# One more Strassen pair in the second half of an attention output projection, and a memory load moved to a later step

## The chip, the cores and the metric

The kernel runs on one core of a Trainium2 chip. The core has five engines that each work through a queue of their own in order: TensorE (PE, matrix products into PSUM), VectorE (DVE) and ScalarE (ACT) for elementwise work, GpSimd (POOL) and SyncE (SP), which here mainly send DMA transfers. The metric is device microseconds (us) of one execution. Before the change the median of 3 runs is 2434.72 us (2434.51 to 2436.06).

## The reference

One residual block of an encoder, 256 tokens by 2048 features, all in float32: a SwiGLU feed-forward net, a mixer, a cross attention to 256 memory tokens, a second feed-forward net, each followed by a layer norm. The change lies at the end of the mixer, where its two attention branches A and B are projected, gated, added and projected again, and in the layer norm of the memory that is prepared beside it:

```python
g_a, g_b = jnp.split(g, 2, axis=-1)                  # sigmoid gates, 256 x 2048 each
y_b = mla_attention(...) @ w_o_b                      # 256 x 2048 by 2048 x 2048
mix = (g_a * y_a + g_b * y_b) @ w_out
h = layer_norm(ALPHA * h + mix)
m = layer_norm(mem, mem_ln_g, mem_ln_b)               # keys and values of the cross attention
```

## The kernel before

**Precision.** Every float32 operand is split into a rounded part `hi` and a rest `lo`; a product is three matmuls (hi hi, hi lo, lo hi). ScalarE makes `hi` of a weight tile by two casts of 1024 columns (L264), VectorE makes `lo` by a subtraction over all 2048 columns (L267). A weight tile is 128 x 2048 (1 MB), loaded by SyncE into one of three `raw` buffers (L193); two `hi` and two `lo` buffers hold the parts. A buffer is reused when its last reader has finished, so a load waits for the subtraction of the tile three before, and a cast for TensorE two tiles back.

**Pairs and groups.** `pair_group` computes a 256 x 1024 piece of a projection. One weight tile holds two tiles of the inner dimension (a pair) for two blocks of 512 output columns. The inner dimension of 2048 makes eight pairs, called 0 to 7 here. A plain pair (`mm_pair`, L311) is 2 inner tiles x 2 token halves x 2 column blocks x 3 = 24 matmuls of 512 columns. A Strassen pair (`mm_sums`, L366) makes the same products with 7 instead of 8 block products, 21 matmuls. For it VectorE adds weight blocks into a stage tile (L248 over 1024 columns, L250 twice over 512), ScalarE casts it in two halves (L264, `H5<-X3`), VectorE subtracts it (L267, `X2<-X3,H5`); the tile's own `hi` and `lo` then span 1536 columns. It also needs a `form`, sums of the activations (`sum_forms`, L321 and L325, split at L255 and L256), kept either in a named block or in four small work tiles, which are soon reused. Its shared results collect in four extra PSUM banks, the other four than those of the group's plain results; `shared` (L679 to L684) combines them.

**B's projection.** `out_b(g)` runs two groups, g = 0 and 1. The table `AT_YB` says which pairs are Strassen pairs: 2, 4 and 6 in the first group, 4 and 6 in the second. The forms of 4 and 6 lie in block T0; that of 2 lies in work tiles. The activations of B lie in blocks T2 (pairs 0, 1), T3 (2, 3), H4 (4, 5) and T1 (6, 7). After a group `done` (L1282 to L1284) adds the shared results, multiplies by the gate and adds branch A; plane copies (L846, ScalarE), DMA transposes (L850, SyncE) and joins (L854, L255, L256) then turn the result into blocks for the next projection. The first group's turning runs beside the second group; the second group's runs beside `w_out`, whose first pairs read the first group's blocks X0 and X1.

**Memory.** `mem_norm` returns steps that are woven between the pairs of the `w_out` groups. Step 0 loads the memory as tokens (two 1 MB tiles into T1 and T2) and turned (two 1 MB tiles into T3 and H4), all from GpSimd's queue. Each waits until B's second group has read the block. Steps 10 to 14 use the turned memory.

**Order.** The program states the work in one sequence with priorities; a scheduler that models the engines places each instruction in its engine's queue when the program is built. So an added instruction can also change the order of its neighbours.

Of the kernel before, what the change touches and what calls it, by code (L numbers as in the profile page):

```python
# [30 lines left out]
            {3: ("X1", 0), 5: ("X1", 1), 7: ("X0", 0)})  # L31
SUMS_GATE, AT_GATE = {**SUMS_IN, 5: ("F", 0)}, ((2, 4, 5, 6), (2, 4, 5, 6), (2, 4, 6), (2, 4, 6))
ORDER_GATE = (0, 2, 1, 4, 5, 3, 6, 7)
SUMS_YB = {4: ("T0", 0), 6: ("T0", 1), 2: None}
AT_YB = (2, 4, 6), (4, 6)
SUMS_XQ = {4: ("H5", 0), 6: ("H5", 1), 2: None}
SUMS_XV = {4: ("T3", 0), 6: ("T3", 1), 2: None}
SUMS_XO = {2: None, 4: ("H2", 0), 6: ("H2", 1)}
# [63 lines left out]
class Kernel:  # L102
# [767 lines left out]
    def mixer(self, xT, st, steps):  # L870
# [403 lines left out]
        def out_b(g):  # L1274
# [21 lines left out]
            def turn(n):  # L1296
                def fn():
                    mix.blocks += self.act([("X0", "X1", "T0", "X3")[2 * g + n]]).blocks
                    for tt in range(2):
# [4 lines left out]
                return fn  # L1304
            self.pair_group(g, t["w_o_b"][g], 512, KT, lambda: oB["t"], AT_YB[g], fb, ps, qs, None,
                            (("H5", "X2"), "X3"))
# [8 lines left out]
        for c in (2, 4, 6):  # L1315
            self.add(self.forms_step(fb, SUMS_YB, c, lambda: oB["t"]))
        side = out_b(0)
# [13 lines left out]
    def mem_norm(self):  # L1331

        nc, t = self.nc, self.t
        e = self.mem = {}

        def load():
            e["m"] = [self.block(f"T{1 + tt}", (P, D)) for tt in range(2)]
            e["raw"] = [self.block(g) for g in ("T3", "H4")]
            for j in range(2):
                nc.gpsimd.dma_start(e["m"][j], t["mem"][j])  # L1340
            for j in range(2):
                nc.gpsimd.dma_start(e["raw"][j], t["memT"][:, 8 * j:8 * j + 8, :])

        def stat(tt):
            def fn():
                if tt == 0:
                    e["diag"] = self.w2((P, 4, P))
                    e["ones"] = self.w1((P, P))
                    nc.gpsimd.memset(e["ones"], 1.0)
                st = self.ln_begin()  # L1350
                with self.tc.issue_after(self.last_lo.ins):
                    for n in range(4):
                        self.ln_piece(st, e["m"][tt], n)
                kept = self.chain
                mean, r, _ = self.ln_scale(st)
                self.chain = kept
                for k, v in enumerate((mean, r)):
                    nc.vector.tensor_scalar(e["diag"][:, 2 * k + tt, :], self.ident, v, None, ALU.mult)
                if tt:
                    e["mT"] = self.act(["H0", "H1", "H2", "H3"])  # L1360
            return fn

        def spread():

            ps = self.at_tile()
            with self.tc.issue_after(self.last_mm.ins):
                for j in range(4):
                    nc.tensor.matmul(ps[:, j * P:(j + 1) * P], e["ones"], e["diag"][:, j, :], start=True, stop=True)
            e["mr"] = self.w2((P, 2, 1, S))
            nc.scalar.copy(e["mr"].rearrange("p a o s -> p (a o s)"), ps)  # L1370

        def quarter(q):
            def fn():
                v = e["raw"][q // 2][:, q % 2 * 4:q % 2 * 4 + 4, :]
                for k, op in enumerate((ALU.subtract, ALU.mult)):
                    nc.vector.tensor_tensor(v, v, e["mr"][:, k].to_broadcast([P, 4, S]), op)
                for j in range(4):
                    kt = 4 * q + j
                    nc.scalar.activation(v[:, j, :], v[:, j, :], AF.Identity,
                                         bias=self.vec("mem_ln_b", kt), scale=self.vec("mem_ln_g", kt))  # L1380
                self.split(v, e["mT"].blk(0, 4 * q, 4), e["mT"].blk(1, 4 * q, 4))
            return fn

        return {0: [load], 4: [stat(0)], 7: [stat(1)], 9: [spread], 10: [quarter(0)], 11: [quarter(1)], 13: [quarter(2)], 14: [quarter(3)]}

    def turned_norm(self, ln, st, x):

# [289 lines left out]
def _pairs(u, g, n, turned):  # L1677


    import numpy as np  # L1680
    k, c = u.shape
    w = np.stack([m.reshape(k // P, P, c // n, n) for m in (u, g)])
    for j in range(c // n):
        for i in turned[j]:
            w[:, 2 * i:2 * i + 2, :, j] = w[::-1, 2 * i:2 * i + 2, :, j].copy()
    return w.transpose(3, 2, 1, 0, 4).reshape(c // n, P, k // P * 2 * n)


def _halves(w):

    w = w.reshape(w.shape[0], -1, 2, 512)
    return [w[:, :, i].reshape(w.shape[0], -1) for i in (0, 1)]
# [6 lines left out]
def _layout(i):  # L1699
# [39 lines left out]
    r["w_o_a"] = _pairs(*_halves(a["w_o_a"][0]), 512, [(), ()])  # L1739
    r["w_o_b"] = _pairs(*_halves(a["w_o_b"][0]), 512, AT_YB)  # L1740
    r["w_out"] = _pairs(*_halves(a["w_out"][0]), 512, [(), ()])
# [35 lines left out]
```

## Time and profile before

| | |
|---|---|
| Median of 3 runs | 2434.72 us |
| The profiled execution | 2432.88 us, of which the span of the instructions is 2431.0 us |
| TensorE busy | 2422.4 us |
| VectorE busy | 2131.3 us (88%) |
| ScalarE busy | 1553.1 us (64%) |
| B's second group on TensorE | 1241.62 to 1283.78 us |
| Granted TensorE clock | 1.0 of full speed |

The busy time of TensorE is modelled from its queue, so "100%" says that it never stood empty for long, not that it runs at its peak. What another engine's time costs is read from the stretch in which it works and from who waits for whom there.

### The profile page before, as it was taken

The page shows a single profiled execution, that of the slowest core. Times are in us where ns is not written, and L with a number is a line of the kernel's source. Part 1 is how long each engine was busy: PE and PEld are TensorE (multiplying, and loading weights), DVE is VectorE, ACT ScalarE, POOL GpSimd, SP SyncE. Part 2 cuts the span into 40 slices and gives each one's busy share as a digit, 9 for nine tenths or more (in the row PEclk, how much of TensorE's full clock was granted, in tenths as well). Part 3 has the DMA queues.
Part 4 walks back from the last instruction along what each step waited for, and adds up shares of the span by engine and source line. Part 5 has one row for each costly group of instructions (what it writes and reads, how often), then busy time and mean ns, then how long its engine had stood idle before and what let it go on. Part 6 is the DMA issues. An engine that isn't in the chain of part 4 may idle for free.

```text
span 2431.0 us, 29704 instructions
## 1 busy us (share of the span) xinstructions
PE 2422.4 (100%) x11280; PEld 2021.5 (83%) x11280; DVE 2131.3 (88%) x2437; ACT 1553.1 (64%) x2022; POOL 36.0 (1%) x81
## 2 busy tenths in 40 slices
PE   9999999999999999999999999999999999999999
PEld 8888888889888888888888888888888888888887
DVE  8999989899889998789788889879879999888997
ACT  6676745666555557878565787755666675556662
POOL 0000000000000001000000000000000000000000
PEclk9999999999999999999999999999999999999999
DMA  7766656667645657776577577655556766666665
GB/s 267 253 211 215 206 201 223 210 202 230 218 174 211 216 202 242 236 203 176 186 254 246 170 237 214 216 183 192 191 199 213 228 222 211 219 207 207 201 222 180
DMA packets 176416, 516.21 MB, mean 212 GB/s; under 512 B 111729, under 2 KB 112497, under 8 KB 121105
## 3 DMA queue, kind: packets, MB, share of 16 engines
q1 hardware_dynamic: 170816, 495.83, 61.5%
q0 software_dynamic: 4592, 17.30, 2.3%
q8 instruction: 88, 1.44, 0.2%
q10 hardware_dynamic: 864, 1.18, 0.1%
q14 instruction: 56, 0.45, 0.1%
HBM read 485.30 MB, written 2.10 MB: 200 GB/s over the span
## 4 chain that ended last, share of the span: by engine, by line
PE 89%; DVE 4%; ACT 3%; DMA 2%; issue 1%; SPq 0%; DVEq 0%; ACTq 0%
PE at L311 25%; PE mm L311 24%; PE at L366 11%; PE mm L366 11%; PE mm L298 10%; PE mm L277 4%; PE mm L279 2%; DVE lo L267 2%; ACT hi L264 2%; PE at L1034 1%; DMA raw<-w_xq 1%; DMA raw<-w_xk 0%; DMA raw<-w_xv 0%; PE at L1088 0%; ACT w L832 0%
## 5 line engine op out<-in xcount | busy, mean ns | idle before, releaser
L264 ACT CAST hi<-raw 128x1024 fp32r<-128x1024 f32 (+1 forms) x852 | 803.4, 980 | 440.4 <-PE at L311 130.5
L267 DVE TENSOR_TENSOR lo<-raw,hi 128x2048 fp32r<-128x2048 f32 (+1 forms) x427 | 902.2, 2115 | 136.1 <-ACT hi L264 129.1
L311 PE MATMUL mm<-hi,T 128*128 128x512 f32 (+1 forms) x1312 | 308.1, 384 | 0.5 <-ACT hi L255 0.4
L264 ACT CAST X<-H 128x1024 fp32r<-128x1024 f32 (+1 forms) x170 | 174.7, 1034 | 171.5 <-DVE H L248 117.5
L311 PEld LDWEIGHTS mm<-hi,T 128*128 128x128 f32 x1312 | 244.4, 188 | 46.8 <-ACT hi L255 0.9
L311 PE MATMUL at<-hi,T 128*128 128x512 f32 x1136 | 272.3, 390 | 0.0
L311 PEld LDWEIGHTS at<-hi,T 128*128 128x128 f32 x1136 | 213.3, 188 | 44.4
L267 DVE TENSOR_TENSOR X<-H,X 128x2048 fp32r<-128x2048 f32 (+1 forms) x85 | 191.5, 2253 | 62.1 <-ACT X L264 61.9
L311 PE MATMUL mm<-lo,T 128*128 128x512 f32 (+1 forms) x656 | 158.1, 383 | 0.0
L311 PE MATMUL at<-lo,T 128*128 128x512 f32 x568 | 141.0, 390 | 0.0
L311 PEld LDWEIGHTS mm<-lo,T 128*128 128x128 f32 x656 | 122.2, 188 | 22.4
L311 PE MATMUL at<-hi,H 128*128 128x512 f32 x560 | 133.4, 390 | 0.0
L311 PEld LDWEIGHTS at<-lo,T 128*128 128x128 f32 x568 | 106.7, 188 | 22.1
L311 PEld LDWEIGHTS at<-hi,H 128*128 128x128 f32 x560 | 105.0, 188 | 21.5
L250 DVE TENSOR_TENSOR H<-H,raw 128x512 f32<-128x512 f32 (+1 forms) x170 | 115.7, 681 | 2.4
L311 PE MATMUL mm<-hi,H 128*128 128x512 f32 x480 | 115.6, 392 | 0.4 <-DVE w L684 0.4
L311 PEld LDWEIGHTS mm<-hi,H 128*128 128x128 f32 x480 | 89.6, 188 | 19.5 <-DVE w L684 0.8
L248 DVE TENSOR_TENSOR H<-raw 128x1024 f32<-128x1024 f32 (+1 forms) x85 | 102.2, 1203 | 0.5 <-DMA raw<-w_gate 0.3
L366 PE MATMUL mm<-X,X 128*128 128x512 f32 x342 | 91.3, 392 | 0.0
L264 ACT CAST X<-raw 128x1024 fp32r<-128x1024 f32 (+1 forms) x54 | 55.4, 1035 | 48.7 <-DVE raw L250 38.7
L366 PE MATMUL at<-X,X 128*128 128x512 f32 (+1 forms) x315 | 82.7, 386 | 0.0
L854 ACT COPY w<-w 128x1024 uint16<-128x1024 uint16 (+1 forms) x60 | 75.6, 1273 | 1.5 <-DMA w<-w 1.4
(387 smaller groups left out, 4153.9 us busy)
## 6 DMA issues: line engine op xcount, KB each, us to landing
raw<-ffn_w_in SPq DMA_DIRECT2D x150, 1024.0 KB, 4.9
raw<-ffn_w_out SPq DMA_DIRECT2D x66, 1024.0 KB, 4.9
raw<-w_gate SPq DMA_DIRECT2D x32, 1024.0 KB, 4.7
raw<-ffn_w_out_r SPq DMA_DIRECT2D x16, 1024.0 KB, 5.0
raw<-w_qk SPq DMA_DIRECT2D x16, 1024.0 KB, 5.3
raw<-w_o_b SPq DMA_DIRECT2D x16, 1024.0 KB, 4.8
raw<-w_out SPq DMA_DIRECT2D x16, 1024.0 KB, 5.1
raw<-w_xk SPq DMA_DIRECT2D x16, 1024.0 KB, 5.3
```

The source lines that it names most:

```text
L248: self.nc.vector.tensor_tensor(two[0], two[1], raw[:, :m].unsqueeze(1).to_broadcast([P, 2, m]), ALU.add)
L250: self.nc.vector.tensor_tensor(t[:, a * m:a * m + m], t[:, b * m:b * m + m], raw[:, a * m:a * m + m], ALU.add)
L264: self.last_hi = self.nc.scalar.copy(hi[:, c:d], src[:, c:d])
L267: self.last_lo = self.nc.vector.tensor_tensor(lo[:, :n], src, hi[:, :n].bitcast(F32), ALU.subtract)
L277: self.nc.tensor.matmul(ps, hi[j], x.both(kt), start=(j == 0), stop=False)
L279: self.last_mm = self.nc.tensor.matmul(ps[:, :S], lo[j], x.at(0, kt), start=False, stop=(j == n - 1))
L298: self.last_mm = self.nc.tensor.matmul(ps, x.at(xi, kt)[:, tt * P:(tt + 1) * P], w[wi][:, j * 512 + c:j * 512 + c + m], start=(start and j ...
L311: self.last_mm = self.nc.tensor.matmul(ps[tt, g][:, :n], x.at(xi, kt)[:, tt * P:(tt + 1) * P], w[wi][:, c:c + n], start=first and j + wi + ...
L366: self.last_mm = self.nc.tensor.matmul(bank[:, :m], a[xi], v[wi][:, c * m:(c + 1) * m], start=own and first and wi + xi == 0, stop=own and ...
L854: self.nc.scalar.copy(self.words(u, n).rearrange("p (c k) -> p k c", k=2), self.words(s, n).rearrange("p (k c) -> p k c", k=2))
L1034: nc.tensor.matmul(ps[:, c0:c0 + nk], q[:, tt * P:(tt + 1) * P], k[:, :nk], start=(j == 0), stop=(j == len(parts) - 1))
```

## The change

The second group's pair 2 becomes a Strassen pair, with the weights laid out accordingly. The form of pair 2 now lies in block F, which the gates' projection used for a fourth pair earlier, so that it survives from the first group to the second. The load of the turned memory leaves step 0 of `mem_norm` and becomes a step of its own, 5.

```diff
-SUMS_YB = {4: ("T0", 0), 6: ("T0", 1), 2: None}
-AT_YB = (2, 4, 6), (4, 6)
+SUMS_YB = {4: ("T0", 0), 6: ("T0", 1), 2: ("F", 0)}
+AT_YB = (2, 4, 6), (2, 4, 6)
...
             e["m"] = [self.block(f"T{1 + tt}", (P, D)) for tt in range(2)]
-            e["raw"] = [self.block(g) for g in ("T3", "H4")]
             for j in range(2):
                 nc.gpsimd.dma_start(e["m"][j], t["mem"][j])
+
+        def load_turned():
+            e["raw"] = [self.block(g) for g in ("T3", "H4")]
             for j in range(2):
                 nc.gpsimd.dma_start(e["raw"][j], t["memT"][:, 8 * j:8 * j + 8, :])
...
-        return {0: [load], 4: [stat(0)], 7: [stat(1)], 9: [spread], 10: [quarter(0)], 11: [quarter(1)], 13: [quarter(2)], 14: [quarter(3)]}
+        return {0: [load], 4: [stat(0)], 5: [load_turned], 7: [stat(1)], 9: [spread], 10: [quarter(0)], 11: [quarter(1)], 13: [quarter(2)], 14: [quarter(3)]}
```

VectorE's queue where the first group of B ends and the second's pairs 1 and 2 are prepared (`raw_9959`, `raw_10008` and `raw_10039` are pairs 1, 2 and 3; H_933 is a gate block of the first group), before:

```order
L1282 TENSOR_TENSOR w_1573_9928<-w_1573_9928,mm_9691 128x512
L267 TENSOR_TENSOR lo_9962<-raw_9959,hi_9961 128x2048
L1283 TENSOR_TENSOR H_933_6171<-H_933_6171,w_1573_9928 128x512
L267 TENSOR_TENSOR lo_10011<-raw_10008,hi_10010 128x2048
L1284 TENSOR_TENSOR H_933_6171<-H_933_6171 128x2x512
L267 TENSOR_TENSOR lo_10042<-raw_10039,hi_10041 128x2048
```

and with the change (pairs 1, 2 and 3 are `raw_9950`, `raw_9957` and `raw_10039`):

```order
L1282 TENSOR_TENSOR w_1570_9919<-w_1570_9919,mm_9682 128x512
L267 TENSOR_TENSOR lo_9953<-raw_9950,hi_9952 128x2048
L1283 TENSOR_TENSOR H_933_6171<-H_933_6171,w_1570_9919 128x512
L250 TENSOR_TENSOR X_1575_9959<-X_1575_9959,raw_9957 128x512
L1284 TENSOR_TENSOR H_933_6171<-H_933_6171 128x2x512
L250 TENSOR_TENSOR X_1575_9959<-X_1575_9959,raw_9957 128x512
L267 TENSOR_TENSOR lo_10006<-raw_9957,hi_10005 128x1536
L267 TENSOR_TENSOR X_1583_10011<-X_1575_9959,H_1582_10010 128x2048
L267 TENSOR_TENSOR lo_10042<-raw_10039,hi_10041 128x2048
```

Pair 2 now has four entries here in place of one, and a fifth, its L248, stands further up, between L682 and L683 of the first group. The subtraction for pair 3 stands behind all of them.

ScalarE's queue where pair 6's stage tile (into H_1604) and pair 7's weights (`raw_10193` before, `raw_10190` now) are cast, before:

```order
L264 CAST H_1604_10157<-X_1597_10121 128x1024 x2
L255 CAST X_1606_10162<-H_885_5874 128x4x128
L854 COPY H_933_6171<-H_933_6171 128x2x512 x2
L255 CAST X_1610_10200<-H_933_6171 128x4x128
L264 CAST hi_10195<-raw_10193 128x1024 x2
```

and with the change:

```order
L264 CAST H_1604_10154<-X_1601_10122 128x1024
L264 CAST hi_10192<-raw_10190 128x1024 x2
L264 CAST H_1604_10154<-X_1601_10122 128x1024
L854 COPY H_933_6171<-H_933_6171 128x2x512
L679 COPY w_1614_10232<-mm_10054 128x512
L255 CAST X_1610_10197<-H_933_6171 128x4x128
L854 COPY H_933_6171<-H_933_6171 128x2x512
```

The second half of pair 6's stage tile has moved behind the casts of pair 7's weights; pair 4's has moved behind those of pair 5 in the same way.

GpSimd's queue, the four memory loads, as the difference prints them (- before, + now):

```order
-L1340 DMA T_1622_10291<-mem 128x2048
-L1342 DMA T_1623_10292<-memT 128x2048
-L1342 DMA H_1624_10293<-memT 128x2048
-L1340 DMA T_1621_10290<-mem 128x2048
+L1339 DMA T_1622_10288<-mem 128x2048
+L1344 DMA T_1651_10486<-memT 128x2048
+L1344 DMA H_1652_10487<-memT 128x2048
+L1339 DMA T_1621_10287<-mem 128x2048
```

The four stand in the same order as before; only line and buffer numbers differ. In SyncE's queue, too, loads and DMA transposes stand in the order they had.

## Rows read from the trace of the kernel before

**Rows 1.** The profile page: busy us by engine; shares of the chain that ended last.
```profile
PE 2422.4 (100%) x11280; PEld 2021.5 (83%) x11280; DVE 2131.3 (88%) x2437; ACT 1553.1 (64%) x2022; POOL 36.0 (1%) x81
...
PE 89%; DVE 4%; ACT 3%; DMA 2%; issue 1%; SPq 0%; DVEq 0%; ACTq 0%
```

**Rows 2.** Stretches of 10 us around the second group: busy us by engine (x instructions), clock, DMA.
```profile
1240.00:1250.00 10.00, 10.00 (x45) 8.27 (x44) 9.35 (x12) 5.90 (x6) 0.00 (x0) 1.00 0.27 88
1250.00:1260.00 10.00, 10.00 (x46) 8.28 (x45) 9.41 (x8) 7.42 (x8) 0.53 (x1) 1.00 1.00 328
...
1270.00:1280.00 10.00, 10.00 (x46) 8.30 (x45) 9.17 (x8) 9.05 (x12) 0.53 (x1) 1.00 0.98 365
1280.00:1290.00 10.00, 10.00 (x46) 8.29 (x45) 9.86 (x14) 4.40 (x5) 0.53 (x1) 1.00 0.59 211
```

**Rows 3.** TensorE's timeline: start us, us, engine, line, operation.
```profile
1252.50 3.79 PE L311 MATMUL at<-hi,T 128*128 128x512 f32 x16
...
1257.94 3.79 PE L311 MATMUL at<-hi,T 128*128 128x512 f32 x16
...
1263.38 0.61 PE L366 MATMUL at<-hi,H 128*128 128x512 f32 x2
...
1268.14 3.79 PE L311 MATMUL at<-hi,H 128*128 128x512 f32 x16
```

**Rows 4.** VectorE's timeline; in brackets the idle time before and what ended it.
```profile
1237.70 0.68 DVE L681 TENSOR_TENSOR w<-w,at 128x512 f32<-128x512 f32 x1
...
1241.14 1.28 DVE L1282 TENSOR_TENSOR w<-w,mm 128x512 f32<-128x512 f32 x2 [0.64 <-PE mm L311]
...
1246.47 2.29 DVE L267 TENSOR_TENSOR lo<-raw,hi 128x2048 fp32r<-128x2048 f32 x1
...
1255.13 1.22 DVE L248 TENSOR_TENSOR X<-raw 128x1024 f32<-128x1024 f32 x1
1256.38 1.42 DVE L250 TENSOR_TENSOR X<-X,raw 128x512 f32<-128x512 f32 x2
1258.21 1.76 DVE L267 TENSOR_TENSOR lo<-raw,hi 128x1536 fp32r<-128x1536 f32 x1 [0.41 <-PE at L311]
...
1264.44 1.23 DVE L248 TENSOR_TENSOR X<-raw 128x1024 f32<-128x1024 f32 x1 [2.27 <-DMA raw<-w_o_b]
...
1275.69 2.29 DVE L267 TENSOR_TENSOR lo<-raw,hi 128x2048 fp32r<-128x2048 f32 x1 [0.82 <-ACT hi L264]
...
1288.85 2.29 DVE L267 TENSOR_TENSOR lo<-raw,hi 128x2048 fp32r<-128x2048 f32 x1
```

**Rows 5.** ScalarE's timeline, same stretch.
```profile
1252.84 2.00 ACT L846 COPY H<-H 128x1024 uint16<-128x1024 uint16 x2
...
1261.93 2.00 ACT L264 CAST hi<-raw 128x1024 fp32r<-128x1024 f32 x2 [2.09 <-DMA raw<-w_o_b]
...
1273.66 2.00 ACT L264 CAST hi<-raw 128x1024 fp32r<-128x1024 f32 x2
```

**Rows 6.** SyncE's queue, same stretch: loads and DMA transposes it issues.
```profile
1254.30 1.27 SPq L193 DMA_DIRECT2D raw<-w_o_b  x2
1255.61 8.63 SPq L850 DMA_TRANSPOSE H<-H  x2
1264.66 0.33 SPq L193 DMA_DIRECT2D raw<-w_o_b  x1
```

**Rows 7.** GpSimd's queue, same stretch.
```profile
1264.09 0.54 POOL L1342 DMA_DIRECT2D T<-memT  x1 [10.59 <-ACT hi L264]
1274.04 0.53 POOL L1342 DMA_DIRECT2D H<-memT  x1 [9.41 <-PE at L311]
```

**Rows 8.** DMA issues from 1200 to 1345 us: count, KB each, median us to landing.
```profile
raw<-w_o_b SPq DMA_DIRECT2D x12, 1024.0 KB, 5.3
...
H<-H SPq DMA_TRANSPOSE x8, 5.9
```

**Rows 9.** The operations on w_o_b: time from issue to landing.
```profile
DMA to landing us min/median/max: 4.6/4.8/9.1
```

## The prediction

> **What bounds the kernel now.** I read the page first. TensorE counts as busy for 2422.4 of 2431.0 us and holds 89% of the chain that ended last [rows 1], so only TensorE's own work, or a hole newly torn into it, moves the time. Second, the stretches around B's second group: TensorE 10.00 of 10 us in each at granted clock 1.00, and beside it VectorE 9.35, 9.41, 9.17 and 9.86 of 10 [rows 2]. The reader is to see two engines that are both nearly full: work taken from one is put on the other. Third, TensorE's timeline prices a pair. Plain pair 3 starts at 1257.94 and Strassen pair 4 at 1263.38, so a plain pair is 5.44 us, 24 matmuls of 0.227. Pair 5 starts at 1268.14, so a Strassen pair is 4.76 us, 21 times the same [rows 3]. Last, VectorE's timeline shows what slack is left: its idle times from 1237.70 to the start of the subtraction for the second pair of `w_out` at 1288.85 are 0.64, 0.41, 2.27 and 0.82, together 4.14 us [rows 4].
>
> **The change part by part.** *Fewer matmuls.* Pair 2 of the second group goes from 24 to 21: 5.44 - 4.76 = 0.68 us less on the bounding engine. That is the whole gain to be had.
>
> *More on VectorE and ScalarE.* For pair 2 VectorE did one subtraction over 2048 columns, 2.29 us. Now it does L248 (1.22), two L250 (1.42 together), a subtraction over 1536 columns (1.76) and one over 2048 (2.29) [rows 4]: 6.69, so 4.40 us more against 4.14 of idle time, and TensorE comes 0.68 earlier. The cover is therefore just used up and the margins of single tiles decide. ScalarE gains a cast of 512 and one more of 1024, about 1.6 us; it has 2.6 and 0.95 us free in its two fullest stretches [rows 2], and costs something through its order more than through its sum. Bounds for what VectorE's extra costs TensorE: nothing, if all idle time can be moved (nothing excludes it), and 4.4 us, if none can. Between them I walk the new order with the durations of before.
>
> 1. L248 goes in ahead of L683. The eight operations of `done`, 5.33 us from 1241.14 to 1246.47 [rows 4], then start at about 1241.9. The subtraction for pair 1 follows at 1247.2 and ends at 1249.5; TensorE wants it eight matmuls ahead of 1252.50 [rows 3], at 1250.7. Covered.
> 2. Behind it come L1283, L250, L1284 and L250 (512 columns as L681, 0.68; 1024 as L248, 1.22 [rows 4]; each starts some 0.05 ahead of the last one's end), until 1252.5; the subtraction over 1536 ends at 1254.2. TensorE wants it seven matmuls into pair 2, 1254.1. With some 0.06 for the signal: **0.2 us**.
> 3. The second half of the stage tile is cast behind two plane copies (2.00 together, [rows 5]), which start when L1284 ends at 1251.9: cast until 1254.9, stage subtraction until 1257.2, wanted twenty matmuls into pair 2, also 1257.2: **0.05 us**.
> 4. Then follow subtraction 3, L248, subtraction 4, two L250, subtraction 5 and stage subtraction 4, each with its row in [rows 4]: 1268.1. TensorE wants the last one 23 matmuls into pair 4, which now starts at 1262.9: 1268.2. Nothing, without any margin.
> 5. The same count for pair 6 gives 1278.4 against 1278.6. Nothing.
> 6. VectorE next needs the joins of the first group's second gate block, for which ScalarE is ready only at 1280.0, having cast pair 7 and pair 6's half first; then L681, L682, the subtraction for `w_out`'s pair 0, L683 and L684, until 1285.5. L684 frees the fourth PSUM bank that `w_out` writes. TensorE reaches it seven matmuls into `w_out`, at 1284.9: **0.6 us**. Before, the subtraction stood behind L684, not ahead of it.
> 7. `done` again, 5.33 us, and the subtraction for `w_out`'s pair 1 end at 1293.0, which is when it is wanted: **0.07 us**.
>
> Together 0.9 us of new waits against 0.68 saved: +0.2 us. The profiled execution took 2432.88, so 2433.1; the median shown is 1.84 above that execution, which gives **2435.0 us** as a median.
>
> *Form in F.* One cast and one subtraction over 512 columns replace four of each over 128. The block is free since the gates; TensorE reads the form 40 us later. Nothing.
>
> *The memory loads.* Their order in GpSimd's queue is unchanged. The turned halves left at 1264.09 and 1274.04 [rows 7], right after pairs 3 and 5 had been read (pair 4 starts at 1263.38; pair 6 one plain pair after 1268.14, [rows 3]). B's last reads still gate them, so they leave about half a microsecond earlier or later, as TensorE does. Bounds: nothing either way, since their first reader is step 10 of `w_out`: pairs 5, 6 and 7 and ten plain pairs from 1268.14 on, at about 1338, some 60 us after the second load, and a load here lands in 5 to 9 us [rows 8, 9].
>
> *Loads and DMA transposes.* SyncE sends pair 5's load, pair 6's, the transposes of the first group's second gate block, then pair 7's load. Before, pairs 5 and 6 left at 1254.30 as two issues, the transposes held the queue for 8.63 us from 1255.61, and pair 7 left at 1264.66 [rows 6]. Now pair 6's load waits for subtraction 3, which ends at 1259.4, so the transposes are sent at about 1259.8. Fewer transfers are then in flight, so I take 5 us for the transposes instead of 8.63, pair 7 leaves at 1264.8 and lands by the median of 5.3 us [rows 8] at 1270.1, ahead of the 1271.8 at which ScalarE turns to it.
>
> At this place a rule speaks the other way. The rows show a transpose of a quarter megabyte (128x1024 words of 16 bits, [rows 5]) landing after 5.9 us against 5.3 for a whole megabyte loaded, and two of them holding the queue for 8.63 [rows 6, 8]. The Trainium skill, page "Advanced Engine Details and Errata", section "X-Bar Transpose (TRN2)", holds that transposing DMAs are as fast as ordinary ones; if so, pair 7's load would leave a microsecond earlier than I take it and the last rival below would be void. This trace does not agree, so that rival keeps its chance.
>
> **The rivals.** *Full cover.* The waits of steps 2 to 7 do not come, as now at pairs 4 and 6, whose stretches are 10.00 of 10 on TensorE [rows 2]. Against it: no `done` stands between the subtractions there, and VectorE still has idle time. It gives 2434.72 - 0.68 = 2434.0.
>
> *The load does not move.* The order says this is so for the load's half of the change; had it moved, it would ease DMA traffic between 1264 and 1281. For a gain TensorE would have to wait for a weight there, and it does not in any row. It adds nothing to either sum.
>
> *Late load, slower.* Pair 7's load goes out late because pair 6's waits for VectorE and the transposes behind it hold SyncE's queue as long as before: 1259.8 + 8.63 = 1268.4, landing 4.6 to 9.1 us later [rows 9], 1273.0 to 1277.5. It decides from 1271.8 on, because pair 6's second half is cast behind pair 7's weights and that half is wanted four microseconds later: a landing at 1273.0 adds 1.2 us to the sum, at 1275.2 3.3, at 1277.5 5.6. Pair 5's load has the same form: ScalarE already waited 2.09 us for it [rows 5], and pair 4's second half now stands behind it; landing a microsecond late costs one. For it: these waits exist already (VectorE 2.27 for pair 6's load). Against it: each transfer now has fewer beside it. Taken at 1275.2: 2435.0 + 3.3 = 2438.3; at the worst 2440.6, or with pair 5's microsecond 2441.6.
>
> **How the numbers follow.** My forecast has 0.60, full cover 0.24, the late load 0.14, something unnamed 0.02. A measurement of this kernel tells a change from none beyond about 0.2%, 4.9 us: below 2429.9 or above 2439.6. The forecast and full cover lie within. Of the late load's 0.14 about 0.03 lies above 2439.6; the unnamed is shared between the sides. So faster 0.02, same 0.94, slower 0.04. The range: the two quick cases at 2434.0 and 2435.0, widened downwards by half a microsecond for the spread of the three runs (0.2 below and 1.3 above their median), and upwards to the middle of the late load: 2433.4 to 2438.4.
>
> **What would show it.** TensorE's rows from 1241 to 1300: pair 2 in 4.76 us plus a gap of about 0.2 ahead of its `lo` matmuls, and a gap of half a microsecond a third of the way into `w_out`'s first pair. VectorE without idle time beyond 1 us from 1241 to 1293. GpSimd's loads of turned memory at 1263 to 1265 and 1273 to 1275. SyncE's second pair of transposes from about 1260, over by 1265. I am wrong if TensorE shows no gap there (full cover), if a cast of pair 5 or 7 waits for its load while TensorE stands still (late load), or if time changes outside this stretch.

## The result and the profile of the changed kernel

| | before | changed |
|---|---|---|
| Median | 2434.17 us (22 executions, 2432.83 to 2436.17) | 2437.20 us (22 executions, 2434.86 to 2447.66) |
| Ratio | | 1.0019, 95% interval 1.0013 to 1.0025 |
| The profiled execution | 2432.88, span 2431.0 us | 2435.13, span 2433.3 us |

The changed kernel is slower: 3.0 us by the medians, 4.6 by the ratio. The median lies inside the range I gave, but I had forecast no difference, and there is one. The single times say more than the median: 12 of the 22 lie between 2434.9 and 2437.6, ten between 2439.3 and 2447.7. The kernel before has no such second heap: over the whole study 132 executions of it were timed, and one (2438.70) is above 2438.5. So two things have to be explained: a usual execution that is some 2 us long instead of equal, and the ten that are 5 us and more.

The profiled execution belongs to the usual ones. The page of the changed kernel, the lines that answer to [rows 1]:

```profile
PE 2423.5 (100%) x11277; PEld 2019.7 (83%) x11277; DVE 2135.2 (88%) x2438; ACT 1554.4 (64%) x2021; POOL 36.0 (1%) x81
...
PE 86%; DVE 5%; ACT 4%; DMA 2%; issue 2%; SPq 0%; DVEq 0%; ACTq 0%
```

Three matmuls fewer, and still TensorE's busy time is 1.1 us more, since a matmul that waits in the middle of a run of them counts as busy. The gaps have to be read from the starts. TensorE's timeline of the changed kernel (start, us, engine, line, operation), to be laid beside [rows 3]:

```profile
1242.59 3.79 PE L311 MATMUL at<-hi,T 128*128 128x512 f32 x16
...
1253.47 0.61 PE L366 MATMUL at<-hi,T 128*128 128x512 f32 x2
...
1257.32 0.84 PE L311 MATMUL at<-hi,T 128*128 128x512 f32 x3
...
1263.97 0.62 PE L366 MATMUL at<-hi,H 128*128 128x512 f32 x2
...
1274.27 1.07 PE L366 MATMUL at<-hi,T 128*128 128x512 f32 x4
...
1284.91 1.75 PE L311 MATMUL mm<-hi,X 128*128 128x512 f32 x7
1286.82 2.34 PE L311 MATMUL mm<-hi,X 128*128 128x512 f32 x9 [0.15 <-DVE w L684]
...
1290.81 3.79 PE L311 MATMUL mm<-hi,X 128*128 128x512 f32 x16
...
1301.75 3.79 PE L311 MATMUL mm<-hi,X 128*128 128x512 f32 x16
...
1307.88 1.46 PE L311 MATMUL mm<-hi,T 128*128 128x512 f32 x4 [0.53 <-ACT T L255]
```

A Strassen and a plain pair together are 4.76 + 5.44 = 10.20 us without a wait. Pairs 2 and 3 take 10.50, pairs 4 and 5 10.30, pairs 6 and 7 10.64: 0.84 us of waits against 0.68 saved. `w_out`'s first pair takes 5.90 instead of 5.44 (0.46), its second 5.50 (0.06). That is 0.7 us net where the walk of the prediction has 0.2, and 0.44 of it was lost in pairs 6 and 7, where the walk has nothing. From the start of its fourth pair, 1301.75, to that of its fifth, 1307.88, are 6.13 us, another 0.69, and there the prediction has no step at all: the last row waits for the first block that the *second* group's turning makes, T0. ScalarE in the changed kernel ahead of that point:

```profile
1298.27 1.99 ACT L846 COPY H<-H 128x1024 uint16<-128x1024 uint16 x2 [5.18 <-DVE H L1284]
1300.33 2.00 ACT L264 CAST hi<-raw 128x1024 fp32r<-128x1024 f32 x2
1302.87 2.01 ACT L264 CAST hi<-raw 128x1024 fp32r<-128x1024 f32 x2 [0.55 <-DMA raw<-w_out]
1304.78 2.57 ACT L854 COPY H<-H 128x1024 uint16<-128x1024 uint16 x2
1307.22 1.13 ACT L255 CAST T<-H 128x512 fp32r<-128x512 f32 x2
```

`done`, the plane copies and the joins come later than before because VectorE has more ahead of them, and the joins (L854) now stand behind two pairs of casts. By this place the profiled execution has lost 1.4 us. Another 0.97 was lost ahead of 1243 us, before the second group starts; over all traces of this study the second group starts between 1241.4 and 1243.8, with either kernel, so this need not be the change.

SyncE's and GpSimd's queues in the changed kernel, to be laid beside [rows 6] and [rows 7]:

```profile
1255.54 5.10 SPq L193 DMA_DIRECT2D raw<-w_o_b  x2
1260.68 5.08 SPq L850 DMA_TRANSPOSE H<-H  x2
1266.18 0.33 SPq L193 DMA_DIRECT2D raw<-w_o_b  x1
...
1264.68 0.53 POOL L1344 DMA_DIRECT2D T<-memT  x1 [10.22 <-ACT hi L264]
1274.73 0.53 POOL L1344 DMA_DIRECT2D H<-memT  x1 [9.52 <-PE at L311]
```

Here the forecast of the queue holds: the second pair of transposes is sent 5 us later than before (1255.61), because pair 6's load in front of it waits for VectorE, and it takes 5 us. But the turned memory load has stayed at 1264.7. Before, it was sent when the transposes had all but left the queue (1264.09; they left it at 1264.24). Now it is sent a microsecond before they leave it (1265.76). The packets in the two traces show a smaller shift. The transposes' own packets start only when the weight loads ahead are nearly through, at 1263.15 before and at 1264.81 now, and take 2.5 us in both; so the memory load is sent 0.9 us behind their first packet in the one and 0.1 us ahead of it in the other.

### The profile page after: what moved, and what is told of

Its sections match the earlier page's. It is cut to its first block, busy times and chain, and to the rows that moved or that the text cites. A ratio compares the mean times of both kernels' runs of the same rounds, so it can differ in the third digit from the quotient of the medians.

```text
span 2433.3 us, 29699 instructions
## 1 busy us (share of the span) xinstructions
PE 2423.5 (100%) x11277; PEld 2019.7 (83%) x11277; DVE 2135.2 (88%) x2438; ACT 1554.4 (64%) x2021; POOL 36.0 (1%) x81
## 4 chain that ended last, share of the span: by engine, by line
PE 86%; DVE 5%; ACT 4%; DMA 2%; issue 2%; SPq 0%; DVEq 0%; ACTq 0%
PE at L311 24%; PE mm L311 23%; PE at L366 11%; PE mm L366 11%; PE mm L298 10%; PE mm L277 3%; DVE lo L267 2%; ACT hi L264 2%; PE mm L279 2%; PE at L1034 1%; ACT H L854 1%; DMA raw<-w_xq 0%; DMA raw<-w_xk 0%; DMA raw<-w_xv 0%; PE at L1088 0%
## 5 line engine op out<-in xcount | busy, mean ns | idle before, releaser
L248 DVE TENSOR_TENSOR H<-raw 128x1024 f32<-128x1024 f32 (+1 forms) x85 | 102.1, 1202 | 0.7 <-DMA raw<-w_gate 0.4
L854 ACT COPY w<-w 128x1024 uint16<-128x1024 uint16 (+1 forms) x60 | 75.6, 1274 | 1.5 <-DMA w<-w 1.5
```

The costliest lines, as they stand in the source:

```text
L248: self.nc.vector.tensor_tensor(two[0], two[1], raw[:, :m].unsqueeze(1).to_broadcast([P, 2, m]), ALU.add)
L854: self.nc.scalar.copy(self.words(u, n).rearrange("p (c k) -> p k c", k=2), self.words(s, n).rearrange("p (k c) -> p k c", k=2))
```

## The experiments

**Which half of the change, and is it the end of the second group?** The theories when these runs were made: the moved load does nothing; the third pair brings its waits; and the long executions come either from the late joins at T0, in `w_out`'s fifth pair, or from late loads inside the second group.

e1: the pair without the moved load (the edit to `mem_norm` taken back; all five queues then hold what they hold in the changed kernel).

> Only the third Strassen pair; the turned memory is loaded in step 0 as before. On all five engines the instructions stand in the order they have in the changed kernel. Theory A (the pair does it all, the moved load does nothing): median 2435 to 2441, 1 to 6 us over before, with runs up to 10 us apart, as the changed kernel has them. Rival B (the moved load costs something, by its place or its buffers): at most 0.7 us off before, and all runs within 3 us.

2435.28 us against 2433.06, ratio 1.0016 (1.0007 to 1.0025); 5 of 12 executions above 2438.5.

e2: the moved load without the pair (the two tables as before).

> Only the moved load; the second group keeps pairs 4 and 6. Theory A: the time of before, within 1 us, runs within 3 us of each other, memory loads sent at 1253, 1264, 1274 and 1284 us as before. Rival B: 2 us or more over before.

2433.77, ratio 1.0003 (0.9995 to 1.0012), no long execution in 10. The change is its pair; its other half does nothing that these executions can tell, as predicted.

e3: the changed kernel, in which `w_out`'s pairs 4 to 7 multiply the blocks X0 and X1 again instead of T0 and X3, so that nothing waits for the second group's joins. The second half of the mix is left out of the product.

```diff
-                self.out_pair(g, t["w_out"][g], g, KT, lambda: mix, (), None, True, st)
+                self.out_pair(g, t["w_out"][g], g, KT, lambda: Act(mix.blocks[:2] * 2), (), None, True, st)
```

> The changed kernel, but pairs 4 to 7 of w_out read blocks X0 and X1 of B's first group again instead of T0 and X3 of the second, so TensorE no longer waits for the second group's turning (which is still done); this leaves the second half of the mix out of the result. VectorE, ScalarE, SyncE and GpSimd have the same instructions in the same order. Theory C (the cost above my sum and the scattered runs come from the second group's joins arriving late at w_out's pair 4): no gap of TensorE at 1307 us, median about 2434.9, 1 us or more under the changed kernel, runs within 3 us. Rival D (they come from late loads of pairs 5 and 7 and the edges inside the second group): runs still scatter over 5 to 12 us and the median stays at 2436 to 2438.

2435.60, ratio 1.0016 (1.0007 to 1.0024), with 2441.55 and 2443.29 among 11. The late joins do not make the long executions. Nor do they show in the usual ones: TensorE's rows have no wait left at this place, yet the nine lie between 2433.6 and 2437.8, no lower than e1's seven usual ones (2434.1 to 2435.4).

e4: the changed kernel once more, for another profile.

> The changed kernel once more, for a second profile of it. Its runs scatter from 2434.9 to 2447.7. If this one is among the longer: theory C has the added time in one gap ahead of w_out's pair 4 (the joins into T0), of more than the 0.53 us of the first profile; rival D has it in gaps inside B's second group, between 1253 and 1286 us. If it is among the shorter, the rows are those of the first profile within 0.3 us.

It was a long one, 2441.43 us, and shows where the time goes. TensorE, ScalarE and SyncE in it:

```profile
1268.44 0.73 PE L366 MATMUL mm<-H,T 128*128 128x512 f32 x2 [0.66 <-ACT H L264]
...
1282.72 0.73 PE L366 MATMUL mm<-H,T 128*128 128x512 f32 x2 [3.68 <-ACT H L264]
...
1274.35 1.05 ACT L264 CAST H<-X 128x1024 fp32r<-128x1024 f32 x1 [0.58 <-PE at L311]
1279.73 1.99 ACT L264 CAST hi<-raw 128x1024 fp32r<-128x1024 f32 x2 [4.32 <-DMA raw<-w_o_b]
1281.62 1.04 ACT L264 CAST H<-X 128x1024 fp32r<-128x1024 f32 x1
...
1261.41 8.73 SPq L850 DMA_TRANSPOSE H<-H  x2
1270.57 0.34 SPq L193 DMA_DIRECT2D raw<-w_o_b  x1
```

This is the late-load rival, row by row. The transposes hold the queue for 8.73 us, pair 7's load leaves at 1270.57 and lands 9.1 us later; ScalarE, which casts it at 1279.73, has waited 4.32 us for it; pair 6's second half, queued behind, is cast at 1281.62, and TensorE stands still for 3.68. Over four executions of this order the loss follows ScalarE's wait for this load: waits of 0.36 (the changed kernel's first profile), 0.56 (e1), 1.22 (e3) and 4.32 us (e4), and pairs 6 and 7 are 0.44, 0.62, 1.27 and 5.62 us longer than 10.20. In the first three TensorE waits where it reads the subtracted stage tile, in e4 already where it reads the half cast last. The stretches of 5 us of e4 (busy us of TensorE and its weight loads, VectorE, ScalarE, GpSimd; granted clock, DMA share, GB/s) show where the load's time went, and what follows:

```profile
1260.00:1265.00 5.00, 5.00 (x24) 4.13 (x23) 4.97 (x5) 1.82 (x2) 0.00 (x0) 1.00 0.98 372
1265.00:1270.00 5.00, 4.34 (x20) 3.26 (x19) 3.89 (x3) 3.63 (x5) 0.54 (x1) 1.00 1.25 78
1270.00:1275.00 5.00, 5.00 (x23) 3.99 (x22) 4.39 (x5) 4.39 (x6) 0.00 (x0) 1.00 1.24 229
...
1280.00:1285.00 5.00, 2.28 (x8) 1.83 (x9) 3.25 (x2) 5.00 (x7) 0.00 (x0) 0.88 0.99 406
1285.00:1290.00 5.00, 5.00 (x19) 3.98 (x18) 4.16 (x6) 3.99 (x5) 0.00 (x0) 0.78 0.73 300
```

With a busy share above 1.2 (packets stand open for long) the DMA engines move 78 GB/s from 1265 to 1270. The same stretch of the changed kernel's first profile has 348:

```profile
1265.00:1270.00 5.00, 5.00 (x24) 3.94 (x23) 5.00 (x3) 4.97 (x6) 0.22 (x1) 1.00 1.15 348
```

The second loss is the clock. TensorE, having stood still for 3.68 us, gets 0.88 and 0.78 of full speed in the next two stretches, a part of each at the lower level of 1.2 GHz. From pair 7's first cast to the first matmul of `w_out` are 11.51 us in the first profile, 11.48 in e1 and 11.46 in e3, all three at a clock of 1.00, and 12.01 in e4 (1279.73 to 1291.74): the clock costs some 0.5 us there, by this estimate. Pairs 4 to 7 together take 27.07 us in e4, from 1264.67 on, and 20.94 in the first profile: 6.1 us more, and e4's span is 6.2 us longer.

**Order on the engines, or traffic?** Four edits: two that move the order in the changed kernel, one that puts the order alone into the kernel before, and one that takes traffic away.

e5, in `load`, for pairs 3, 5 and 7 of the second group:

```diff
+                if i and isinstance(queue[i - 1], Sums) and queue[i - 1].first:
+                    first = self.last_hi
```

> The changed kernel with one rule more for ScalarE: in B's second group the casts of a plain pair's weights (pairs 3, 5, 7) are issued behind both stage casts of the Strassen pair ahead of it; nothing is left out. Late-load theory (pair 7's weights land 7 to 9 us after they are sent, their casts wait for them, and pair 6's second half, queued behind, holds TensorE; in the long execution the wait was 4.32 us and TensorE's gap 3.68): the gaps at pair 6's second half and the one at pair 4's go, no execution is more than 4 us above the quickest, ratio 0.9997 to 1.0006 against 1.0019 for the change. Rival (the third pair itself or something outside the second group makes the long executions, and the order on ScalarE does not matter): a third to a half of the executions stay 4 to 10 us long, ratio 1.0012 to 1.0025.

A miss: 2437.95 us, ratio 1.0029 (1.0014 to 1.0044), 4 of 8 above 2438.5, up to 2450.76. The gap at pair 6's half is indeed gone, though the load was late by 1.64 us, but another has come:

```profile
1277.41 1.05 ACT L267 CAST hi<-raw 128x1024 fp32r<-128x1024 f32 x1 [1.64 <-DMA raw<-w_o_b]
...
1293.52 3.35 PE L314 MATMUL mm<-lo,X 128*128 128x512 f32 x8 [4.73 <-DVE lo L270]
```

The edit also made the scheduler put `w_out`'s first subtraction behind most of `done`, so the run does not answer the question it was made for.

e6, SyncE sends the second pair of transposes behind pair 7's load:

```diff
-            return {2: [send(0)], 4: [send(1)], 5: [turn(0)], 6: [turn(1)]}
+            return {2: [send(0)], 5: [turn(0)], 6: [send(1)], 7: [turn(1)]}
```

> The changed kernel with the DMA transposes of the first group's second gate block sent behind pair 7's weight load in SyncE's queue instead of ahead of it; ScalarE keeps pair 6's second half behind pair 7's casts. Late-load theory: the load leaves some 5 us earlier (near 1261 instead of 1266) and lands before ScalarE turns to it at 1273; no wait for it, no gap at pair 6's second half, no long executions, ratio 0.9998 to 1.0008. If pair 5's load (pair 4's half behind it) makes the long executions instead, they stay. Rival (order and loads do not matter): ratio 1.0012 to 1.0025 with long executions.

2436.46 us, ratio 1.0017 (1.0008 to 1.0026), 2 of 11 above 2438.5: outside what I expected, although pair 7's wait is gone as it should be. The transposes, now from 1263.92, still meet the memory load at 1264 and hold the queue for 7.44 us, and the next load in the queue is late instead:

```profile
1263.92 7.44 SPq L850 DMA_TRANSPOSE H<-H  x2
...
1276.69 1.06 ACT L264 CAST hi<-raw 128x1024 fp32r<-128x1024 f32 x1 [1.80 <-DMA raw<-w_out]
```

This edit too moved more than it says: ScalarE's and VectorE's order changed around `w_out`'s first pair, where TensorE waits 0.78 us for L684 instead of 0.15.

e7, the kernel before with pair 6's second half put behind pair 7's casts:

```diff
+                    if behind:
+                        stage, h, l = behind.pop()
+                        with self.tc.issue_after(self.last_hi.ins):
+                            self.nc.scalar.copy(h[:, 1024:], stage[:, 1024:])
```

> The kernel before, two Strassen pairs in the second group, with one thing of the change put in alone: the second half of pair 6's stage tile is cast behind pair 7's weights. Late-load theory: pair 7's weights landed at 1273.66 in the profile before, so the half would be cast until 1276.7 and subtracted until 1279.0, where TensorE wants it at 1278.1: 0.9 us more in a usual execution and more wherever the load is later; ratio 1.0004 to 1.003, with executions 4 us and more above the quickest. Rival (the order does not matter): ratio within 0.0004 of 1, no long executions.

2435.73 us, ratio 1.0009 (1.0000 to 1.0018). Its profile has the gaps forecast, 0.77 at the half and 1.22 behind it, but none of 11 executions is above 2437.3. The order costs a microsecond or two, at the edge of what 11 executions show; it does not make long executions by itself, as I had expected it to.

e8, the changed kernel with the turned memory loads held back by a small copy that needs the joined gate block:

```diff
             for j in range(2):
+                nc.gpsimd.tensor_copy(e["raw"][j][:, 0, :8], e["gates"][2][:, 0, 0, :8])
                 nc.gpsimd.dma_start(e["raw"][j], t["memT"][:, 8 * j:8 * j + 8, :])
```

> The changed kernel with the two turned memory loads (2 MB) held back until the second group's first gate block is turned, some 35 us later (1304 instead of 1265 and 1275); they are first read at about 1338. This asks who slows the transposes and pair 7's load. If it is the memory loads beside them: the load lands within 6 us, no long executions, ratio at most 1.0006. If it is not (the transposes and weight loads do it among themselves): a third to a half of the executions stay 4 to 10 us long, ratio 1.0010 to 1.0025.

2434.05 us against 2433.22, ratio 1.0006 (0.9997 to 1.0015), 2431.91 to 2436.25: no long execution in 11, with the order of TensorE, VectorE, ScalarE and SyncE untouched. DMA issues from 1255 to 1285, median us to landing, of e4 and then of e8:

```profile
raw<-w_o_b SPq DMA_DIRECT2D x3, 1024.0 KB, 8.6
...
T<-memT POOLq DMA_DIRECT2D x1, 1024.0 KB, 12.0
...
H<-H SPq DMA_TRANSPOSE x3, 11.8
```

```profile
raw<-w_o_b SPq DMA_DIRECT2D x3, 1024.0 KB, 5.4
...
H<-H SPq DMA_TRANSPOSE x3, 6.1
```

**More and less of it.** e9: e8 with the joins of the second group's first gate block put ahead of one pair of casts (`with self.prio(SOON if g and not n else 0):` around the join).

> The changed kernel with the turned memory loads held back as in the last run of the series before, and the joins of the second group's first gate block given priority on ScalarE, so that they stand ahead of the casts for pair 4 of the output product, as in the kernel before. Collision theory (the memory loads collide with the transposes and with pair 7's load; behind that only small waits are left, the largest 0.35 to 0.53 us at the first read of T0): no long executions, and 0.3 to 0.5 us quicker than with the held loads alone: 2433.0 to 2434.0 with before at 2433.2, ratio 0.9998 to 1.0005. Rival (the third pair makes long executions by itself and their absence last time was chance): a third of the executions above 2439.

2435.66, ratio 1.0008 (1.0000 to 1.0017); again no long execution in 11. Slower than expected: the joins did not help. The profile shows 1.17 us of waiting at the same place, T0's first reads, now for VectorE's subtraction (L256); why that is late was not followed further.

e10: the kernel before with the loads held in the same way.

> The kernel before with its two turned memory loads held back in the same way, nothing else. Both theories: no change, ratio within 0.0005 of 1. If the held loads are worth a microsecond to the kernel before as well, then what they took from the changed kernel is not all owed to the third pair.

2433.45, ratio 1.0001 (0.9992 to 1.0009). The memory loads cost the kernel before nothing that shows.

e11 and e12: the changed kernel and the kernel before, each with one plain memory load made twice.

```diff
-            for j in range(2):
+            for j in (0, 1, 1):
                 nc.gpsimd.dma_start(e["m"][j], t["mem"][j])
```

> The changed kernel with 1 MB more of memory traffic: the first plain memory load is made twice, the second time when the first has landed, so at about 1260, beside the second pair of transposes. Collision theory: pair 7's load is late more often and by more; over half of the executions 4 us and more above the quickest, median 2439 to 2446, ratio 1.0025 to 1.006. Rival (traffic beside the transposes does not matter): as the changed kernel, ratio 1.0012 to 1.0025.

> The kernel before with the same extra 1 MB at the same place. Collision theory: there pair 6's halves stand ahead of pair 7's casts, and pair 7's weights, cast at 1273.7, are wanted only at 1278.3, so up to some 2.5 us of lateness cost nothing: ratio 0.9998 to 1.0012, few or no long executions. Rival (the margin is the same and traffic does it in either kernel): the same long executions as the changed kernel with the extra load.

e11 is 2445.20 us, ratio 1.0059 (1.0033 to 1.0085), as expected. e12 is not: 2449.41, ratio 1.0066 (1.0054 to 1.0078), none of 5 executions under 2444. TensorE in e11, its granted clock around the gap, and then ScalarE and TensorE in e12:

```profile
1286.29 1.22 PE L366 MATMUL mm<-H,T 128*128 128x512 f32 x2 [9.66 <-ACT H L264]
...
1275.00:1280.00 5.00, 1.62 (x8) 1.00 (x6) 0.00 (x0) 0.00 (x0) 0.00 (x0) 1.00 0.99 247
1280.00:1285.00 5.00, 0.00 (x0) 0.00 (x0) 0.00 (x0) 1.70 (x2) 0.00 (x0) 0.60 1.01 415
1285.00:1290.00 5.00, 3.71 (x9) 2.94 (x10) 4.68 (x3) 5.00 (x7) 0.00 (x0) 0.50 0.89 320
1290.00:1295.00 5.00, 5.00 (x21) 4.04 (x20) 3.90 (x5) 3.25 (x5) 0.00 (x0) 0.87 0.33 136
```

```profile
1281.60 1.33 ACT L854 COPY H<-H 128x1024 uint16<-128x1024 uint16 x1 [6.15 <-DMA H<-H]
...
1286.53 1.99 ACT L264 CAST hi<-raw 128x1024 fp32r<-128x1024 f32 x2 [3.13 <-DMA raw<-w_o_b]
...
1287.62 5.46 PE L311 MATMUL at<-hi,T 128*128 128x512 f32 x16 [6.95 <-ACT hi L264]
```

In e12 pair 6's halves are in time, as they should be by the order before, but pair 7's own weights land 18 us after they are sent, and the few microseconds of margin are nothing against that. With enough traffic beside the transposes the kernel before has long executions too, so the order of its casts (e7) is not what kept it free of them. That it was *when* its transposes ran fits, but no run moves that alone in the kernel before.

**By order alone, by time alone.** In e13 one thing moves on one queue: the transposes go ahead of pair 6's load, so they no longer wait for VectorE.

```diff
+            if self.hook and i + 1 < len(queue) and isinstance(queue[i + 1], Sums): self.hook.pop()()
             form_sums(i + 1)
...
-            return {2: [send(0)], 4: [send(1)], 5: [turn(0)], 6: [turn(1)]}
+            return {2: [send(0)], 3: [lambda: self.hook.append(send(1))], 5: [turn(0)], 6: [turn(1)]}
```

> The changed kernel with one move on one queue: SyncE sends the second pair of transposes right behind pair 5's load, ahead of pair 6's load, which waits for VectorE; nothing else in any engine's order moves. The transposes then start near 1256 as in the kernel before, instead of near 1261, and should be over (5 us) before the first turned memory load is sent at 1264.7; pairs 6's and 7's loads leave at about 1261 to 1262. If the collapse comes of transposes and a memory load in flight together: no long executions, ratio 0.9999 to 1.0007. If total traffic in the stretch is what counts, whatever its order: a third of the executions stay 4 us and more above the quickest, ratio 1.0010 to 1.0025.

2434.63 us against 2433.24, ratio 1.0006 (0.9997 to 1.0014), none of 11 above 2437.13. SyncE and GpSimd in e13:

```profile
1255.43 7.70 SPq L851 DMA_TRANSPOSE H<-H  x2
1263.23 1.46 SPq L193 DMA_DIRECT2D raw<-w_o_b  x2
...
1264.21 0.54 POOL L1345 DMA_DIRECT2D T<-memT  x1 [10.18 <-issue]
```

The transposes are not quicker (7.70 us), they have left the queue when the memory load is sent. Pair 7's load is also sent earlier than in the changed kernel, so e13 alone does not tell which of the two helps; e8 and e14, which leave SyncE's order as it is, do. e14 holds the loads only until about 1280 (the copy reads the first group's second gate block instead):

> The changed kernel with the turned memory loads held only until the first group's second gate block is joined (about 1278 instead of 1304), so until the transposes and pair 7's load are over; the loads then run beside those of the output product. If the collapse comes of transposes and a memory load in flight together: no long executions, ratio 1.0000 to 1.0008, as with the long hold (1.0006). If total traffic counts: the loads of the output product are late instead, with waits on them, ratio 1.0010 to 1.0025.

2435.43, ratio 1.0007 (0.9998 to 1.0016), one of 11 above 2438.5 (2439.40). e15 does both, e8's long hold and e13's order:

> Both: transposes ahead of pair 6's load, and the turned memory loads held until 1304. By the collision theory the quietest form of the changed kernel: no long executions, at best the full gain of the pair less the small waits at T0 and at the fourth bank: ratio 0.9997 to 1.0005. If the third pair costs time by itself: 1.0005 or above.

2434.11, ratio 1.0005 (0.9996 to 1.0013), none of 11 above 2437.51.

Together: with the third pair and the memory load sent while the transposes are in the queue (the changed kernel, e1, e3, e4) 18 of 46 executions are above 2438.5; e5 and e6, where this is so too but other orders moved, add 6 of 19. With the two kept apart by order or by time (e8, e9, e13, e14, e15) it is 1 of 55, with the same pair and the same bytes. So the turned memory load beside the transposes makes the long executions. What is left, 0.8 to 2.4 us by these five medians, is in part the waits read off above: in the first profile, all but pair 7's late load, 0.30, 0.10, 0.46, 0.06 and 0.69, together 1.6 us against 0.68 saved, so 0.9 net. That accounts for e8 and e15; no run takes these waits away one by one, and what e9 and e14 have above it is not explained. The five intervals overlap, so no order among them is shown. No form of the third pair beat the kernel before.

## Why the prediction was wrong

*Steps 1 to 7.* Nearly right in size, and in place but for pair 2. Forecast 0.25 for pairs 2 and 3, measured 0.30; but 0.2 of the forecast stood ahead of the `lo` matmuls (step 2), and there TensorE does not wait at all: its first 17 matmuls of pair 2, 1253.47 to 1257.32, take 17 times 0.227. All of the 0.30 comes where it reads the subtracted stage tile, for which step 3 had 0.05. That the two sums agree is luck. For pairs 4 and 5 forecast nothing, measured 0.10; at the fourth bank 0.6, measured 0.46 with the row naming L684; at `w_out`'s second pair 0.07, measured 0.06 (5.50). Pairs 6 and 7 lost 0.44 where step 5 has nothing; in e9, whose load was in time, they lost nothing.

*Where the walk ended.* It followed VectorE's delay to `w_out`'s second pair and stopped. The delay went on through `done`, the plane copies, the transposes and the joins to the first read of T0, 0.69 us that no step has. That alone would have made the sum about +0.9 instead of +0.2, though e3 does not show it in the total.

*The step that failed*: "Loads and DMA transposes". I took one number for the transposes, 5 us, and one for the landing behind them, "the median of 5.3 us [rows 8]", which gave 1270.1, and so left the late load to a rival. The transposes did take 5.08 us in the first profile. The 5.3 was the wrong size: it is the median of twelve loads between 1200 and 1345 us, and pair 7's load is not like them. Its own row among the DMA issues (the last number is the time to landing) in the kernel before, e10, the first profile and e8:

```profile
raw<-w_o_b SPq DMA_DIRECT2D x1, 1024.0 KB, 7.6
raw<-w_o_b SPq DMA_DIRECT2D x1, 1024.0 KB, 4.8
raw<-w_o_b SPq DMA_DIRECT2D x1, 1024.0 KB, 7.1
raw<-w_o_b SPq DMA_DIRECT2D x1, 1024.0 KB, 4.7
```

With the turned memory load ahead of it this load lands after 7.6 us before and 7.1 in the changed kernel, with the memory loads held after 4.8 and 4.7. The row of 7.6 was there before the change; before, the load was sent at 1264.66 and had the time. In the first profile it was sent at 1266.18, and ScalarE waited 0.36 us for it; in e4 the transposes held the queue for 8.73, the load landed after 9.1, and ScalarE waited 4.32. The reason that I gave for the 5 us, "Fewer transfers are then in flight", holds for the loads ahead of the transposes, not for the memory load at 1264.7 beside and behind them. I had written down both times, 1259.8 for the one and about 1264 for the other, in two paragraphs, and never laid them side by side.

*The memory loads.* "Bounds: nothing either way, since their first reader is step 10" looks only at who reads the loads. What they do to the transfers beside them was not bounded. e8, by its median 0.8 us above the kernel before where the changed kernel is 3.0, and e11 show that this was the larger part.

*The late-load rival* was right as a mechanism, including the queue of casts behind pair 7's weights, and its point of decision was of the right kind; it had 0.14, where ten of 22 executions were long and the one of this kind with a trace, e4, shows it. Its price, 1.2 to 5.6 us, just reaches e4's loss of 5.62 in pairs 6 and 7, but leaves out the clock, some 0.5 us there. Three of the 22 exceed its worst case of 2441.6; no trace of these was kept, so it is open whether their loads landed later still. "Against it: each transfer now has fewer beside it" forgets the memory load in the same way. *Full cover* did not come: the waits of steps 3, 6 and 7 did. Two ends of the range miss their own sums by 0.1 (2433.5 and 2438.3); nothing hangs on it.

*The rule I weighed.* The two transposes move 0.5 MB. In the first profile their packets take 2.5 us, some 210 GB/s, where the two weight loads ahead of them run at 340; until then, from 1260.68 to 1264.81, they wait for these loads. In e4 the DMA engines moved 78 GB/s over 5 us with two transposes and a load in flight. The Trainium skill, page "Advanced Engine Details and Errata", section "X-Bar Transpose (TRN2)", has transposing DMAs as fast as ordinary ones; this case's traces do not agree. The rival kept for that reason is the one that came. The rows that I set against the rule, 5.9 us to landing and 8.63 in the queue, hold such waiting too, so the reason was weaker than it looked. Another page bears on the memory loads: as shown above, a load from GpSimd's queue slows one from SyncE's (7.1 us to landing in the first profile, 4.7 in e8). The Trainium skill, page "DMA: Bandwidth & Descriptors", section "Issuing engines are not separate DMA queues", says that transfers from all issuing engines share the same 16 DMA engines; the trace agrees, and I should have priced the loads by it.

## What to carry to other kernels

When a step moves, list every transfer that is in flight at its new place, whoever issues it and however late its reader is, and price the neighbours too; a load that nobody waits for can delay one that somebody does. Take a transfer's time from its own row, not from the median of others like it. Where a queue has a loose end, follow the delay until something absorbs it, past the end of the stretch that changed. And where a profile of one execution decides by a margin of a microsecond or two, count the other executions: here 18 of 46 fell on the far side.

## What the runs showed of the hardware

DMA transposes with a load beside them sometimes all but stop. The DMA rate from 1255 to 1285 us of e4, in slices of 0.75 us:

```profile
GB/s 199 232 255 428 470 360 372 393 459 371 459 317 295 274 165 17 22 33 22 126 36 45 26 211 454 404 360 514 350 350 524 339 360 481 350 513 360 481 371 306
```

From 1266 to 1272 it is 17 to 126 GB/s, then over 400 again. The profiles of e11 and e12 have such stretches too (slices down to 19 GB/s in each). A short one needs no memory load: e10 has 61 and 23 GB/s from 1263.25 to 1264.75 and e15 24 from 1263.25 to 1264.00, with none in flight, and e13 has 23 from 1261.75 to 1262.50, two microseconds before its memory load is sent.

The packets in e4's trace show what the long one is made of. From 1266.4 to 1269.3 eight packets of pair 6's load, of 8 KB each, move one after the other, all but the first in 0.31 us; then packets of the transposes start again for less than a microsecond, and from 1269.6 to 1272.1 eight packets of the turned memory load move in the same way, one after the other, while the second transpose is not through before 1273.6. In e10, e13 and e15 the first row has some four packets and 1.2 us, and there is no second. An estimate: 8 KB in 0.31 us is 26 GB/s, a sixteenth of the 420 or so that the loads reach at their best, as if one of the 16 DMA engines were behind and the transposes waited for it; the packets do not name their engine, so this is not shown.

What decides whether it happens in a given execution is open. In e4 and in the first profile transposes and memory load are sent at the same distance, 4.0 us, and only e4 has it. And meeting a load is not enough: in all 17 profiles the plain memory load is sent 0.2 to 0.6 us ahead of the first packet of the first pair of transposes, and that pair's packets are through in 2.2 to 2.6 us.

A gap on TensorE costs more than itself. After 3.68 us it was followed by clocks of 0.88 and 0.78 over 5 us each (some 0.5 us lost), after 9.66 us by 0.50 and 0.87. The 0.89 us by which TensorE waited at pair 4's half in e13 had no such sequel: 1.00 in every 5 us around it.
